# One core of a hybrid encoder: rows of the output projection through 32x32 transposes, and another order of the attention halves

## The chip, the cores and the metric

The kernel runs on one core of a Trainium2 chip, in one launch, all in float32 on the outside. The metric is the device time of one execution in microseconds (us); less is better. Engines are named as in the profile: PE (TensorE, with its weight loads as PEld), DVE (VectorE), ACT (ScalarE), POOL (GpSimd), SP (the queue that issues almost all transfers here).

## The reference, cut to what matters

One layer over 1024 rows of width 1024: RMSNorm, one wide projection, two mixers, the output projection with a residual, and an MLP of width 4096 with squared ReLU, then a final RMSNorm.

```
h = rmsnorm(x, norm_mix_g)
z = h @ w_in                      # q, k, v, g, a_f, a_b, su, sv
# mixer A, 4 heads, chunks of 64, forward and backward:
#   state_n+1 = dec_n * state_n + k_n v_n^T ; o = intra(q, k, v) + q_n state_n
o_gla = rmsnorm_head(o_f + o_b) * norm_g * silu(g)
# mixer B, 4 groups, chunks of 128:
o_sgu = gelu(su) * (w_s @ (rmsnorm_group(gelu(sv)) * norm_g) + b_s)
x = x + concat([o_gla, o_sgu]) @ w_out          # called x2 below
h = rmsnorm(x, norm_mlp_g)
x = x + square(relu(h @ w_mlp1)) @ w_mlp2
out = rmsnorm(x, final_norm_g)
```

## The kernel before

Every matmul operand is split into a high and a low part (`split`, L122: ACT writes the high part, DVE the difference), and each product is three matmuls of 128x512 on PE. Weight pieces of 128x512 come through `wpiece` (L132): a transfer by SP into a ring `wr` of two buffers, then the split into `wh` and `wl`, three buffers each.

**Recording and order.** The kernel is recorded in one pass. Instructions of PE keep the order in which they are recorded; those of the other engines are placed by a scheduler, which works with its own model of time and with priorities. The middle of the kernel is driven by a table of events: a generator `stream` records the projections in steps (mostly 12 matmuls, some 2.7 us of PE), and after step n every event with a number up to n is recorded. An event is one stage of one half (512 rows, `hf` 0 or 1) of one head `h`: gate, `st_cum` (cumulated decays), `st_score`, `st_tr`, `st_kv`, `st_attend`, `st_out`; and `sgu_mix`, the mixing matmuls of mixer B for one half and one group.

**State scan.** `st_kv` of the second half of a head runs two chains on DVE over the tile `X`: the forward one (L438) on the lower 64 partitions, and the backward one (L444) on the upper 64, which goes from chunk 14 down to chunk 1 and writes the state of the chunk before each. So the states of the second half of the rows are complete after six of its fourteen steps, those of the first half at its last step. `st_attend` multiplies masked scores `P` with `V` and then `qd` with the states `X` of its half. Its results go through ACT and POOL (norm) and DVE, and `st_out` transposes them back on PE and gates them into `V`. The tiles that PE writes here (`pg`) are a ring of four PSUM banks, handed out in the order of recording: a stage waits until the bank of four stages back has been read, mostly by DVE.

**Output projection.** It is computed transposed: for each of eight blocks `d` of 128 channels, 48 matmuls give two tiles of 128 channels x 512 rows, DVE adds the residual (`x2t[d, hf]`), and for each pair of blocks `x2_combine` (L650) makes the split operands of the MLP (a Winograd form, seven block products instead of eight). The MLP's end needs x2 also row by row, so `x2_natural` (L634) turns each tile with four PE transposes into a `pg` bank, copies it by ACT into a tile `st` of the ring `tmp` (two buffers) and stores it to DRAM as `x2n`, runs of 128 floats. It is recorded after the next block's matmuls; the last one after the first MLP pair (L809). `x2n` is read back by rows, first from L805.

**Start.** SP first loads a piece of `wv`, then `cols` (norm gains), then half a piece of x; the other half comes by ACT's queue (L176). The first matmul needs the split x (ACT, with a gain from `cols`) and the cast weight (DVE, L185).

Of the kernel before, what the change touches and what calls it, by code (L numbers as in the profile page):

```python
# [15 lines left out]
P = 128  # L16
# [15 lines left out]
def tile_encoder(  # L32
# [25 lines left out]
    nc = tc.nc  # L58
# [6 lines left out]
    def sb(tag, bufs, shape=(P, 512), dt=F32):  # L65
        cnt[0] += 1
        home = tiny if tag in ("sm", "rso", "r3") else pool
        return home.tile(list(shape), dt, tag=tag, bufs=bufs, name=f"{tag}{cnt[0]}")

    def one(name, shape, dt=F32):  # L70
        return tiny.tile(list(shape), dt, tag=name, bufs=1, name=name)

    def bank(tag, bufs=4):
        cnt[0] += 1
        return psum.tile([P, 512], F32, tag=tag, bufs=bufs, name=f"{tag}{cnt[0]}")
# [3 lines left out]
    def in_table_order(ins):  # L79

        if table["last"] is not None:
            tc.add_manual_dep(
                ins.ins,
                table["last"].ins.name,
                mybir.DependencyInfo(mybir.DependencyClass.NoSync, mybir.DependencyReason.DATA),
                reason="table order",
            )
        table["last"] = ins
# [11 lines left out]
    def pg():  # L100
        return bank("pg")
# [7 lines left out]
    def transp(o, i):  # L109
        tc.keep_in_program_order(nc.tensor.transpose(out=o, in_=i, identity=cid))  # L110

    def v3(ap, a):
        return ap.rearrange("p (a b) -> p a b", a=a)

    def bcast_in(ap, n):
        return ap[:, None, :].broadcast_to([ap.shape[0], n, ap.shape[1]])
# [15 lines left out]
    def wpiece(src):  # L132
        with tc.high_priority(offset=HP):
            raw = sb("wr", 2)
            nc.sync.dma_start(out=raw, in_=src)
            hi, lo = sb("wh", 3, dt=F32R), sb("wl", 3, dt=F32R)
            split(raw, hi, lo)
        return hi, lo
# [3 lines left out]
    ccols = one("cols", [P, 24])  # L142
# [12 lines left out]
    def in_order(ins, after):  # L155
        if after is not None:
            tc.add_manual_dep(
                ins.ins,
                after.ins.name,
                mybir.DependencyInfo(mybir.DependencyClass.NoSync, mybir.DependencyReason.DATA),  # L160
                reason="order of use",
            )
        return ins

    for k in range(KT):
        for hf in range(2):
            raw = sb("qk", 8)
            a, b = sb("xa", 16, dt=F32R), sb("xb", 16, dt=F32R)
            g = ccols[:, G1 + k : G1 + k + 1]
            xh[k, hf], xl[k, hf] = a, b  # L170
            if k == 0 and hf == 0:
                wraw = sb("wr", 2)
                whi, wlo = sb("wh", 3, dt=F32R), sb("wl", 3, dt=F32R)
                h0, h1 = slice(0, 256), slice(256, 512)
                with tc.high_priority(offset=1000):
                    first = nc.scalar.dma_start(out=raw[:, h0], in_=xT[0, :, h0])  # L176
                    table["last"] = in_order(
                        nc.scalar.preload_act_table_set("natural_log_exp_and_others"), first
                    )
                    table["logexp"] = True  # L180
                    in_table_order(nc.scalar.copy(out=one("wact", [P, 8]), in_=warm[:, 0:8]))
                    lead = nc.sync.dma_start(out=wraw, in_=wv[0])
                    lead = in_order(nc.sync.dma_start(out=ccols, in_=cols), lead)
                    lead = in_order(nc.sync.dma_start(out=raw[:, h1], in_=xT[0, :, h1]), lead)
                nc.vector.tensor_copy(out=whi, in_=wraw)  # L185
                in_table_order(nc.scalar.activation(out=a[:, h0], in_=raw[:, h0], func=AF.Copy, scale=g))
                nc.vector.scalar_tensor_tensor(
                    out=b[:, h0], in0=raw[:, h0], scalar=g, in1=a[:, h0].bitcast(F32), op0=ALU.mult, op1=ALU.subtract
                )
                nc.vector.tensor_tensor(out=wlo, in0=wraw, in1=whi.bitcast(F32), op=ALU.subtract)  # L190
                split(raw[:, h1], a[:, h1], b[:, h1], g)
                wvp.append((whi, wlo))
            else:
                nc.sync.dma_start(out=raw, in_=xT[k, :, hf * 512 : hf * 512 + 512])
                split(raw, a, b, g)
                if hf == 0:
                    wvp.append(wpiece(wv[k]))
# [63 lines left out]
    for hf in range(2):  # L261
        rb = pg()
        for i in range(4):
            t = hf * 4 + i
# [257 lines left out]
    def sgu_mix(hf, g):  # L522
        mx = pg()
        for i in range(4):
            mm(mx[:, i * P : i * P + P], SV[:, hf * 4 + i, g, :], cws[:, g * P : g * P + P], True, True)
        nc.vector.scalar_tensor_tensor(
            out=SV[:, hf * 4 : hf * 4 + 4, g, :], in0=v3(mx, 4), scalar=ccols[:, GS + g : GS + g + 1],
            in1=bcast_in(cbs[:, g * P : g * P + P], 4), op0=ALU.mult, op1=ALU.add,
        )
# [40 lines left out]
    ev = []  # L570
    for h in range(H):
        for hf in range(2):
            u = 2 * h + hf
            b0 = 7 + 6 * u
            for off, fn in ((-3 if u == 2 else -4, gate), (0, st_cum), (4, st_score), (5, st_tr), (7, st_kv)):
                ev.append((b0 + off, fn, h, hf))
            b1 = 7 + 6 * (2 * h + 1) + 11
            ev.append((b1 + hf, st_attend, h, hf))
            ev.append((b1 + 4 + hf, st_out, h, hf))
    for g in range(4):  # L580
        ev.append((21 + g, lambda hf, g: sgu_mix(hf, g), 0, g))
        ev.append((41 + g, lambda hf, g: sgu_mix(hf, g), 1, g))
    ev.sort(key=lambda e: e[0])
    pos = 0
    for _ in stream():
        pos += 1
        while ev and ev[0][0] <= pos:
            _, fn, h, hf = ev.pop(0)
# [6 lines left out]
    for src, base in ((SV, 4), (V, 0)):  # L595
        for j in range(4):
            for hf in range(2):
                a, b = sb("xa", 16, dt=F32R), sb("xb", 16, dt=F32R)
# [32 lines left out]
    x2n = dram.tile([NT, P, D], F32, name="x2n", tag="x2n", bufs=1)  # L631
    x2t = {}

    def x2_natural(d):  # L634
        for hf in range(2):
            tp = pg()
            for i in range(4):
                c = slice(i * P, i * P + P)
                transp(tp[:, c], x2t[d, hf][:, c])
            st = sb("tmp", 2)  # L640
            nc.scalar.copy(out=st, in_=tp)
            nc.sync.dma_start(
                out=x2n[hf * 4 : hf * 4 + 4, :, d * P : d * P + P].rearrange("t p c -> p t c"), in_=v3(st, 4)
            )


    XC = {n: {} for n in ("B11", "B21", "T2", "T1", "T3", "B22", "T4")}
# [30 lines left out]
    for n, d in enumerate(order):  # L678
        banks = [pf(), pf()]
        for p, k0 in ((1, 4), (0, 0)):  # L680
            hi, lo = wpiece(wo[d, p])
            for hf in range(2):
                for kk in range(4):
                    k = k0 + kk
                    a, b = hi[:, kk * P : kk * P + P], lo[:, kk * P : kk * P + P]
# [3 lines left out]
        for hf in range(2):  # L689
            with tc.high_priority(offset=HP):  # L690
                t = sb(("sg", "kn")[n % 2], 2)
# [258 lines left out]
    for p in range(NPAIR):  # L950
# [13 lines left out]
        if 2 <= p < 6:  # L964
            t = 2 + p
# [3 lines left out]
        if 9 <= p < 13:  # L969
            t = p - 9  # L970
# [57 lines left out]
    for tt in range(4):  # L1028
        t = 4 + tt
# [17 lines left out]
    for tt in range(4):  # L1047
        c = slice(tt * P, tt * P + P)
# [93 lines left out]
```

## Time and profile before

| what | us |
|---|---|
| median of 3 runs (lowest, highest) | 1019.59 (1015.92, 1019.97) |
| the profiled execution | 1017.8 |
| its span, first to last instruction | 1016.0 |
| PE busy in the span | 1000.5 (98%) |
| DVE busy | 693.0 (68%) |
| ACT busy | 474.0 (47%) |

The span is 1.8 us shorter than the time of its execution, and that execution lies 1.8 us below the median. PE is busy nearly always, at a granted clock of 0.995 on the mean; so what matters is what PE executes and the few places where it waits. The kernel's parts stand in the trace so: first projection to 48 us, the projections with both mixers to 303 us, output projection to 397 us, first MLP product to about 690 us, second to 1016 us.

### The profile page before, as it was taken

What the parts mean: (1) busy time and instruction counts of PE and PEld (TensorE: products, weight loads), DVE (VectorE), ACT (ScalarE), POOL (GpSimd) and SP (SyncE); (2) the same over time, 40 slices, a digit from 0 to 9 for tenths busy, and PEclk for the clock granted to TensorE, in tenths of its full rate; (3) what the DMA queues carried; (4) which work ended last, traced back from release to release, by engine and by line L of the source; (5) the groups of instructions that cost most, each with busy time, mean ns of one, the idle gap of its engine ahead of it and who ended that gap; (6) DMA issues with size and microseconds to landing.
All of it is one profiled execution on the core that took longest, in us unless ns stands there. A gap on an engine that the chain in (4) does not pass through costs nothing.

```text
span 1016.0 us, 14249 instructions
## 1 busy us (share of the span) xinstructions
PE 1000.5 (98%) x5014; PEld 825.1 (81%) x5014; DVE 693.0 (68%) x1178; ACT 474.0 (47%) x887; POOL 92.6 (9%) x101
## 2 busy tenths in 40 slices
PE   9999999898999999999999999999999999999997
PEld 7887888787888888888888888887888888788885
DVE  6245877776684557877677677665446776799684
ACT  6634646664464446434444433333444444445463
POOL 1001521342220000000000000000000000004031
PEclk9999999999999999999999999999999999999999
DMA  9422111110113444646446445226975652367342
GB/s 307 163 72 74 42 33 63 42 38 26 54 42 123 136 125 134 208 155 218 146 176 214 150 154 177 104 96 232 362 264 178 206 193 69 111 246 263 104 145 83
DMA packets 84984, 145.46 MB, mean 143 GB/s; under 512 B 8881, under 2 KB 17841, under 8 KB 84913
## 3 DMA queue, kind: packets, MB, share of 16 engines
q1 hardware_dynamic: 83760, 142.59, 41.8%
q10 hardware_dynamic: 1152, 1.97, 0.5%
q8 instruction: 39, 0.64, 0.3%
q14 instruction: 33, 0.26, 0.1%
HBM read 106.77 MB, written 37.75 MB: 142 GB/s over the span
## 4 chain that ended last, share of the span: by engine, by line
PE 92%; DVE 5%; ACT 1%; DMA 1%; issue 1%; SPq 0%; POOL 0%; POOLq 0%; DVEq 0%; ACTq 0%
PE pf L106 64%; PE pg L106 27%; PE pg L110 1%; DVE X L444 1%; DVE wl L125 1%; DVE X L438 1%; DMA k<-w 0%; DVE P L403 0%; DMA cols<-cols 0%; DMA wr<-wsv 0%; DVE qk L329 0%; DVE la L343 0%; DVE wl L628 0%; ACT wh L124 0%; DVE kin L382 0%
## 5 line engine op out<-in xcount | busy, mean ns | idle before, releaser
L106 PE MATMUL pg<-xa,xa 128*128 128x512 f32 x768 | 182.5, 390 | 0.4 <-DVE wh L628 0.2
L106 PEld LDWEIGHTS pg<-xa,xa 128*128 128x128 f32 x768 | 144.1, 188 | 31.0 <-DVE wh L628 0.7
L106 PE MATMUL pf<-xa,xa 128*128 128x512 f32 x576 | 138.8, 390 | 0.4 <-ACT kn L792 0.4
L106 PE MATMUL pf<-xa,wh 128*128 128x512 f32 x336 | 136.0, 405 | 0.0
L106 PE MATMUL pf<-xb,wh 128*128 128x512 f32 x336 | 131.9, 392 | 0.0
L106 PEld LDWEIGHTS pf<-xa,xa 128*128 128x128 f32 x576 | 108.0, 188 | 23.3 <-ACT kn L792 0.8
L106 PE MATMUL pf<-xa,wl 128*128 128x512 f32 x320 | 125.6, 393 | 0.0
L124 ACT CAST xa<-xb 128x512 fp32r<-128x512 f32 x76 | 47.1, 621 | 98.2 <-PE pf L106 74.8
L106 PE MATMUL pf<-V,xa 128*128 128x512 f32 x336 | 91.7, 389 | 0.0
L125 DVE TENSOR_TENSOR xa<-xb,xa 128x512 fp32r<-128x512 f32 x76 | 52.3, 689 | 52.8 <-ACT xa L124 52.6
L125 DVE TENSOR_TENSOR wl<-wr,wh 128x512 fp32r<-128x512 f32 x63 | 49.9, 793 | 50.1 <-ACT wh L124 49.8
L106 PEld LDWEIGHTS pf<-xa,wh 128*128 128x128 f32 x336 | 63.9, 190 | 13.9 <-issue 1.2
L941 POOL TENSOR_SCALAR r<-r 128x1 f32<-128x1 f32 x8 | 14.9, 1868 | 657.5 <-ACT tmp L939 657.3
L106 PEld LDWEIGHTS pf<-V,xa 128*128 128x128 f32 x336 | 63.1, 188 | 13.1
L106 PEld LDWEIGHTS pf<-xb,wh 128*128 128x128 f32 x336 | 63.8, 190 | 11.9
L106 PEld LDWEIGHTS pf<-xa,wl 128*128 128x128 f32 x320 | 60.5, 189 | 13.0
L124 ACT CAST wh<-wr 128x512 fp32r<-128x512 f32 x63 | 38.7, 615 | 63.6 <-PE pf L106 54.1
L124 ACT CAST xa<-k 128x512 fp32r<-128x512 f32 x49 | 30.5, 623 | 68.4 <-PE pf L106 66.4
L106 PE MATMUL pf<-xb,xa 128*128 128x512 f32 x192 | 53.9, 389 | 0.0
L106 PE MATMUL pf<-qk,xa 128*128 128x512 f32 x176 | 52.9, 390 | 0.0
L124 ACT CAST xa<-la 128x512 fp32r<-128x512 f32 x34 | 21.1, 622 | 46.5 <-PE pf L106 27.5
L106 PEld LDWEIGHTS pf<-xb,xa 128*128 128x128 f32 x192 | 36.1, 188 | 7.4
(296 smaller groups left out, 1840.4 us busy)
## 6 DMA issues: line engine op xcount, KB each, us to landing
k<-w SPq DMA_DIRECT2D x64, 256.0 KB, 3.1
hA<-kn SPq DMA_DIRECT2D x32, 256.0 KB, 3.1
hS<-wr SPq DMA_DIRECT2D x32, 256.0 KB, 4.3
la<-hA SPq DMA_DIRECT2D x17, 256.0 KB, 5.1
la<-hS SPq DMA_DIRECT2D x17, 256.0 KB, 2.7
qk<-xn SPq DMA_DIRECT2D x16, 256.0 KB, 5.5
wr<-wsv SPq DMA_DIRECT2D x16, 256.0 KB, 2.6
wr<-wo SPq DMA_DIRECT2D x16, 256.0 KB, 2.6
```

Of the source, the lines that this page charges most:

```text
L106: nc.tensor.matmul(out=o, lhsT=lhsT, rhs=rhs, start=start, stop=stop, skip_group_check=more)
L110: tc.keep_in_program_order(nc.tensor.transpose(out=o, in_=i, identity=cid))
L124: nc.scalar.copy(out=hi, in_=src)
L125: return nc.vector.tensor_tensor(out=lo, in0=src, in1=hi.bitcast(F32), op=ALU.subtract)
L438: nc.vector.scalar_tensor_tensor(out=x[lo64, n + 1, :], in0=x[lo64, n, :], scalar=sm[lo64, 2, i : i + 1], in1=v3(kv[i % 2], 4)[lo64, i // ...
L444: nc.vector.scalar_tensor_tensor(out=x[hi64, n - 1, :], in0=x[hi64, n, :], scalar=dec[h, n // 8][hi64, 2, n % 8 : n % 8 + 1], in1=x[hi64, ...
L941: nc.gpsimd.tensor_scalar(out=r[:, 4:5], in0=r[:, 0:1], scalar1=EPS, scalar2=None, op0=ALU.add)
```

## The change

Three edits. At the start, `cols` is loaded ahead of the first weight piece. In the table of events, the two halves of `st_attend` and of `st_out` of each head change places, and the mixing of group g moves from step 21+g to 30+g (first half) and from 41+g to 42+g (second half). In `x2_natural`, the four transposes on PE and the copy by ACT are replaced by one DVE instruction that transposes each 32x32 square of the tile in place of the whole; the four bands of 32 partitions of the result are then stored by a transfer each, which puts every run of 32 floats where it belongs.

```diff
-                    lead = nc.sync.dma_start(out=wraw, in_=wv[0])
-                    lead = in_order(nc.sync.dma_start(out=ccols, in_=cols), lead)
+                    lead = nc.sync.dma_start(out=ccols, in_=cols)
+                    lead = in_order(nc.sync.dma_start(out=wraw, in_=wv[0]), lead)
...
-            ev.append((b1 + hf, st_attend, h, hf))
-            ev.append((b1 + 4 + hf, st_out, h, hf))
+
+            ev.append((b1 + 1 - hf, st_attend, h, hf))
+            ev.append((b1 + 5 - hf, st_out, h, hf))
     for g in range(4):
-        ev.append((21 + g, lambda hf, g: sgu_mix(hf, g), 0, g))
-        ev.append((41 + g, lambda hf, g: sgu_mix(hf, g), 1, g))
+        ev.append((30 + g, lambda hf, g: sgu_mix(hf, g), 0, g))
+        ev.append((42 + g, lambda hf, g: sgu_mix(hf, g), 1, g))
...
         for hf in range(2):
-            tp = pg()
-            for i in range(4):
-                c = slice(i * P, i * P + P)
-                transp(tp[:, c], x2t[d, hf][:, c])
             st = sb("tmp", 2)
-            nc.scalar.copy(out=st, in_=tp)
-            nc.sync.dma_start(
-                out=x2n[hf * 4 : hf * 4 + 4, :, d * P : d * P + P].rearrange("t p c -> p t c"), in_=v3(st, 4)
-            )
+            nc.vector.transpose(out=st, in_=x2t[d, hf])
+            dst = x2n[hf * 4 : hf * 4 + 4, :, d * P : d * P + P].rearrange("t (a i) (b j) -> b i (t a) j", i=32, j=32)
+            for b in range(4):
+                nc.sync.dma_start(out=dst[b], in_=v3(st, 16)[b * 32 : b * 32 + 32])
```

Where the scheduler put things, as the order of the built programs tells it (no times are in it):

On PE, at the attention of the second head, the kernel before has these rows; `qd_1159` is made from the first half of the rows, `qd_1443` from the second, and `X_1457` holds the head's states:

```order
L106 MATMUL pg_1841<-V_490,P_1293 128x128 x4
L106 MATMUL pg_1841<-X_1457,qd_1159 64x128 x8
L110 MATMUL pg_1863<-ident,kd_1655 128x128 x4
...
L106 MATMUL pg_1890<-V_490,P_1576 128x128 x4
L106 MATMUL pg_1890<-X_1457,qd_1443 64x128 x8
L106 MATMUL pg_1912<-cuf,la_1733 64x128
```

and the kernel after these, with the states in `X_1433`; `qd_1419` is of the second half:

```order
L106 MATMUL pg_1841<-V_490,P_1552 128x128 x4
L106 MATMUL pg_1841<-X_1433,qd_1419 64x128 x8
L110 MATMUL pg_1863<-ident,kd_1637 128x128 x4
...
L106 MATMUL pg_1890<-V_490,P_1281 128x128 x4
L106 MATMUL pg_1890<-X_1433,qd_1159 64x128 x8
L106 MATMUL pg_1912<-cuf,la_1727 64x128
```

The halves have changed places; between them stand, in both, the transposes of `kd` and twelve matmuls of the projection.

On DVE, the later part of that head's scan stands so in the kernel before; `sm_1427` is the decay of the second half, `sm_1143` that of the first, L403 masks the scores of the next stage out of their `pg` bank:

```order
L438 SCALAR_TENSOR_TENSOR X_1457<-X_1457,sm_1427,pg_1677 64x128
L347 TENSOR_SCALAR tmp_1735<-la_1733 128x512
L444 SCALAR_TENSOR_TENSOR X_1457<-X_1457,sm_1427 64x128
...
L351 TENSOR_TENSOR la_1733<-la_1733,tmp_1735 128x512
L444 SCALAR_TENSOR_TENSOR X_1457<-X_1457,sm_1143 64x128 x2
L125 TENSOR_TENSOR wl_1978<-wr_1975,wh_1977 128x512
L444 SCALAR_TENSOR_TENSOR X_1457<-X_1457,sm_1143 64x128
L403 COPY_PREDICATED P_1777<-mkf,pg_1779 64x4x64 x2
L444 SCALAR_TENSOR_TENSOR X_1457<-X_1457,sm_1143 64x128
L403 COPY_PREDICATED P_1777<-mkb,pg_1780 64x4x64 x2
L444 SCALAR_TENSOR_TENSOR X_1457<-X_1457,sm_1143 64x128
```

and so in the kernel after, where L526 is the DVE part of `sgu_mix`:

```order
L438 SCALAR_TENSOR_TENSOR X_1433<-X_1433,sm_1403,pg_1665 64x128
L125 TENSOR_TENSOR wl_1804<-wr_1801,wh_1803 128x512
L444 SCALAR_TENSOR_TENSOR X_1433<-X_1433,sm_1403 64x128
L526 SCALAR_TENSOR_TENSOR V_579<-pg_1735,cols,k_577 128x4x128
L347 TENSOR_SCALAR tmp_1729<-la_1727 128x512
...
L351 TENSOR_TENSOR la_1727<-la_1727,tmp_1729 128x512
L444 SCALAR_TENSOR_TENSOR X_1433<-X_1433,sm_1143 64x128 x3
L125 TENSOR_TENSOR wl_1978<-wr_1975,wh_1977 128x512
L444 SCALAR_TENSOR_TENSOR X_1433<-X_1433,sm_1143 64x128
L403 COPY_PREDICATED P_1777<-mkf,pg_1779 64x4x64 x2
L403 COPY_PREDICATED P_1777<-mkb,pg_1780 64x4x64 x2
```

A mixing instruction has come into the scan (one more, L526 of `pg_1698`, stands near its start), and both pairs of L403 now follow its last step.

On SP, one block of the output projection in the kernel before; `wo` are weight pieces, `xT` the residual:

```order
L692 DMA sg_3164<-xT 128x512
L692 DMA sg_3167<-xT 128x512
L642 DMA x2n<-tmp_3091 128x4x128
L135 DMA wr_3311<-wo 128x512
L642 DMA x2n<-tmp_3099 128x4x128
L135 DMA wr_3341<-wo 128x512
```

and in the kernel after:

```order
L642 DMA x2n<-tmp_3166 32x16x32
L690 DMA kn_3240<-xT 128x512
L642 DMA x2n<-tmp_3166 32x16x32 x3
L135 DMA wr_3299<-wo 128x512
L690 DMA kn_3243<-xT 128x512
L642 DMA x2n<-tmp_3172 32x16x32 x4
L135 DMA wr_3329<-wo 128x512
```

Where six transfers were issued for a block there are twelve, and the loads of weights and residual stand among the stores. The DVE transposes (L639) stand directly behind, or within four instructions of, the addition that makes their tile, ahead of later weight splits.

## Rows read from the trace of the kernel before

**Rows 1.** The page: busy time by engine, and the chain that ended last by engine.

```profile
PE 1000.5 (98%) x5014; PEld 825.1 (81%) x5014; DVE 693.0 (68%) x1178; ACT 474.0 (47%) x887; POOL 92.6 (9%) x101
...
PE 92%; DVE 5%; ACT 1%; DMA 1%; issue 1%; SPq 0%; POOL 0%; POOLq 0%; DVEq 0%; ACTq 0%
```

**Rows 2.** Who PE waited for, 100 to 260 us: total, times, longest.

```profile
PE pg L106 <- DVE X L444: 5.5, 2, 2.9
PE pg L106 <- DVE la L343: 0.6, 1, 0.6
```

**Rows 3.** PE in order of time: start, us, what, [idle before, and until what].

```profile
189.47 1.50 PE L106 MATMUL pg<-X,qd 128*64 128x128 f32 x16 [2.65 <-DVE X L444]
...
196.29 1.09 PE L106 MATMUL pg<-X,qd 128*64 128x128 f32 x16
```

**Rows 4.** The chain from 185 to 200 us: start, us, what.

```profile
189.47 1.50 PE pg L106 x16
190.98 1.04 PE pg L110 x4
192.02 3.45 PE pf L106 x12
```

**Rows 5.** The chain from 200 to 440 us.

```profile
208.44 0.44 PE pg L110 x4
...
244.84 1.05 PE pg L110 x4
245.89 3.82 PE pf L106 x12
...
252.50 2.95 PE pf L106 x12
...
325.40 0.87 PE pg L110 x8
```

**Rows 6.** A 5 us stretch: PE, PEld, DVE, ACT, POOL, then PE clock, DMA share, GB/s.

```profile
190.00:195.00 5.00, 5.00 (x27) 4.08 (x22) 3.29 (x6) 3.47 (x12) 1.21 (x2) 0.66 0.17 54
```

**Rows 7.** DVE in the scans of the first and second head.

```profile
131.14 0.75 DVE L526 SCALAR_TENSOR_TENSOR V<-pg,cols,k 128x512 f32<-128x512 f32 x1
...
181.75 0.35 DVE L444 SCALAR_TENSOR_TENSOR X<-X,sm 64x128 f32<-64x128 f32 x1
...
188.26 0.91 DVE L403 COPY_PREDICATED P<-mkb,pg 64x256 f32<-64x256 uint8 x2
189.07 0.35 DVE L444 SCALAR_TENSOR_TENSOR X<-X,sm 64x128 f32<-64x128 f32 x1
```

**Rows 8.** Two blocks of the output projection, columns as in rows 6.

```profile
325.40:337.17 11.77, 11.77 (x58) 9.84 (x57) 8.79 (x15) 7.09 (x13) 0.00 (x0) 1.00 0.45 134
337.17:348.94 11.77, 11.77 (x59) 9.84 (x57) 3.27 (x6) 4.28 (x8) 0.00 (x0) 1.00 0.41 134
```

**Rows 9.** DVE on 128x512: count, ns min/median/max, first and last start.

```profile
L628 DVE TENSOR_TENSOR tmp<-pf,wl x16: 681/692/692, 414.0 to 699.8; 128x512 f32<-128x512 f32 x16
...
L347 DVE TENSOR_SCALAR tmp<-la x8: 406/418/448, 68.7 to 234.6; 128x512 f32<-128x512 f32 x8
```

**Rows 10.** Transfers of 24 to 34 us.

```profile
DMA packets 2170, 3.95 MB, mean 395 GB/s; under 512 B 245, under 2 KB 245, under 8 KB 2169
...
q1 hardware_dynamic: 2169, 3.94, 103.1%
```

**Rows 11.** Transfers of 384.5 to 396.5 us.

```profile
DMA packets 1344, 1.05 MB, mean 87 GB/s; under 512 B 64, under 2 KB 1088, under 8 KB 1344
...
q1 hardware_dynamic: 1344, 1.05, 27.9%
```

**Rows 12.** Issue of one store of x2n by SP.

```profile
338.54 0.38 SPq L642 DMA_DIRECT2D x2n<-tmp  x1
```

**Rows 13.** The chain at the start.

```profile
1.16 3.03 DMA cols<-cols
```

**Rows 14.** DVE at the start.

```profile
3.88 0.57 DVE L185 CAST wh<-wr 128x512 fp32r<-128x512 f32 x1 [3.88 <-DMA wr<-wv]
```

## What the change is predicted to do

> **What bounds the kernel now.** I read the busy shares first: PE has 1000.5 us of work in a span of 1016.0, DVE 693.0, ACT 474.0, and the chain that ended last is PE for 92% and DVE for 5% [rows 1]. The reader is to see that an edit pays here only through what PE executes on that path, and through PE's waits. So I read next for whom PE waits in the mixers, where the table of events is changed: 5.5 us in two waits for the scan (`X`, L444), 0.6 us in one for a gate (`la`, L343) [rows 2]. Then the timeline and the chain around these waits [rows 3 to 7], one block of the output projection [rows 8], and the transfers [rows 10 to 12].
>
> The profiled execution took 1017.8 us (span 1016.0 and 1.8 around it). The sum is made against it; the median of the runs, 1019.59, lies 1.8 higher.
>
> **The order of the halves and the mixing.** In the second head PE is ready for `X` at 189.47 − 2.65 = 186.82 and waits until the scan's last step, 189.07 + 0.35 = 189.42 [rows 3, 7]. But it asks there for the first half, which comes last. The second half's states are complete with the sixth backward step, at 181.75 + 0.35 = 182.10 [rows 7], 4.7 us before PE is ready. So the first attend of the changed kernel doesn't wait. The question is the second one, which now wants the first half.
>
> PE comes to it, counted from 186.82, after an undisturbed attend (1.09), four transposes (0.44) and twelve matmuls (2.95) [rows 3, 5]: 191.3 at the earliest; the `V,P` matmuls ahead of it, and the mixings that now stand before this place, make it later. DVE's scan gets two mixing operations of 0.75 us more and loses the pairs of L403, which stand behind it now; but PE's bank waits for the first of these pairs. One pair takes 0.91 [rows 7]: 189.42 + 2 × 0.75 − 0.91 = 190.0. That leaves 1.3 us. In the third head PE's attend begins at 244.84 − 1.50 = 243.3 after 2.9 us of waiting [rows 2, 3, 5], so it was ready at 240.4 and wants the first half at 244.9; the scan by the same sum is ready at 243.9, 1.0 us earlier. Both waits go: 5.5 us. The first and the fourth head have no such wait before, and none is late enough to get one.
>
> After each of the two stalls the same work takes longer. In the stretch behind the first, PE's granted clock is 0.66 of full speed [rows 6], between its two levels of 1.2 and 2.4 GHz, after 2.65 us without work. The attend takes 1.50 instead of 1.09, the transposes 1.04 instead of 0.44, the twelve matmuls 3.45 instead of 2.95: 1.5 us [rows 3 to 5]. Behind the second the transposes take 1.05 and the twelve matmuls 3.82: 1.5 us [rows 5], the attend not counted. Without a stall the clock has no reason to fall: 3.0 us more.
>
> The 0.6 us wait for a gate belongs to a mixing at step 21 that claims a bank that the gate has not released; with the mixing at step 30 that neighbour is gone. This part gives 5.5 + 3.0 + 0.6 = 9.1 us. The DVE work of the mixing is only moved.
>
> **The rows of the output projection: PE.** Of 64 transposes, eight go together, 0.87 us on the chain [rows 5], eight times: 7.0 us. In a block of 11.77 us PE is busy for 11.77 [rows 8], so nothing else is late there, and a block becomes 10.90. The ACT copies go too, from an engine that is busy for 7.09 and 4.28 of 11.77 us and not on the chain: nothing.
>
> **DVE.** Two transposes of 128x512 per block come in. The trace doesn't show the operation. From below it costs what a one-input operation on this shape takes, 0.42 us; from above, say twice the slowest comparable row, 1.4 us; I take the nearest, 0.69, of a two-input operation [rows 9], since nothing in the trace shows how a square is turned. Blocks carry 8.79 and 3.27 us of DVE work in turn [rows 8]; with 1.4 us more they are 10.2 and 4.7 of 10.9. With 2 × 1.4 the heavy block is 11.6, over its time by 0.7, but two blocks hold 8.79 + 3.27 + 4 × 1.4 = 17.7 of 21.8, and the light one takes up the rest if the splits that DVE makes have so much lead. Cover: DVE's idle time in the light block. The transposes stand right behind the residual additions, and each waits until four stores of the tile two before have landed, one block earlier; behind it on DVE wait the weight splits, and PE for these. A block of 10.9 us is long for landing stores if transfers are not full; that is the next point. The Trainium skill, "VectorE: DVE Perf Modes", section "The three transpose paths", gives 311 ns for 128x128 in bf16 (in squares of 32x32 only); four of them would be 1.24 us, an estimate that no run here shows, two blocks would hold 17.0 of 21.8, and the sum would be the same.
>
> **Transfers.** SP issues twelve transfers a block where it issued six; at 0.38 each [rows 12] that is 4.6 of 10.9 us: nothing, as long as none blocks. The stores' runs shrink from 512 to 128 bytes: 8192 packets become 32768, per block 4096, or 256 on each of 16 engines. The price of such a packet is not in the trace. Where loads of 2 KB fill the engines, 24 to 34 us, 1.031 × 10 × 16 = 165 engine-us over 1924 large packets (2169 − 245) are 86 ns each [rows 10]. At the end of the output projection, 384.5 to 396.5, 0.279 × 12 × 16 = 53.6 engine-us hold 256 packets of 2 KB (22.0) and 1024 of 512 bytes: 31 ns each [rows 11]. A straight line through the two gives 17 ns for 128 bytes, which I take as the lower end, and no gain from shorter runs, 31 ns, as the nearest row. Twice that row, 62, for a short run that is handled in two passes, is the upper end. I take 25, between the line and the row. Per block each engine also carries four loads, 8 packets of 86 ns each, 2.7 us. So the engines are busy for 2.7 + 256 × 0.025 = 9.1 of 10.9 us; at 17 ns 7.1, at 31 ns 10.6, at 62 ns 18.6. It decides from (10.9 − 2.7)/256 = 32 ns. Below that the stores lie beside PE: nothing.
>
> **The start.** `cols` lands at 1.16 + 3.03 = 4.19 [rows 13]; a place earlier it comes by about one issue, 0.4 us, sooner, the weight by as much later. The cast of the weight now runs 3.88 to 4.45 [rows 14]. One of the two operands of the first matmuls gains what the other loses: I take 0; bounds −0.4 and +0.4.
>
> **Sum.** 9.1 + 7.0 + 0 = 16.1: 1017.8 − 16.1 = 1001.7 against the profiled execution, 1019.6 − 16.1 = 1003.5 against the median. I say 1002.5, with its own range of 999 to 1006 (the start, the stretch after stalls, waits of tenths that come anew, and which of the two executions is typical).
>
> **Rivals.**
>
> Second: the waits stay or come back elsewhere. The margins of 1.3 and 1.0 us rest on sums over moved DVE work; if the scheduler's order delays the scan by more (a weight split of 0.7 us and a mixing more), PE waits for the first half, and its clock falls behind the wait. For it: three kinds of DVE work share this stretch, all placed by a model. Against it: `V,P` matmuls and mixings not counted in PE's favour. Only the 7.0 us of the transposes come: 1010.8 against the profile, 1012.6 against the median.
>
> Third: DVE becomes the bound in the output projection. Transposes near 1.4 us, waiting in order for stores, delay splits, and the 7.0 us are lost there while the 9.1 come: 1008.7 to 1010.5. For it: 8.79 us in a heavy block. Against it: 3.27 in the next.
>
> Fourth, on the other side: the short runs make the transfers the bound of the output projection. Its place is SP's order, where weight loads stand among stores, so that PE waits for `wo`. From 32 ns a packet a block grows by 0.256 us for each ns; over eight blocks the 16.1 us saved are used up at about 40 ns ((10.9 − 2.7 + 16.1/8) / 256). At 50 ns a block takes 15.5, 4.6 more than 10.9: eight of them +37, 1017.8 − 16.1 + 37 = 1038.7; at 62 ns +62, 1063. For it: four times as many packets in a direction (store, strided) for which only 512-byte runs are shown. Against it: from 2 KB to 512 bytes the price fell from 86 to 31 ns, so size still counted at 512. The Trainium skill, "DMA: Bandwidth & Descriptors", Specifications, speaks for this rival: below 512 bytes a transfer reads, modifies and writes, and does not reach line rate. No run here shows a run of 128 bytes that fills the engines.
>
> **How the numbers follow.** The forecast 0.68; waits that stay 0.12; DVE bound 0.08; transfers bound 0.12. Up to 1012.5 lie the first, the third and most of the second, so 998 to 1012.5 holds some 0.82; what is left out is nearly all the fourth, which alone would widen the range by 50 us. A measurement of this kernel tells about 0.5% from no change, some 5 us: faster is below 1014.5. The forecast (0.68), the third (0.07) and two thirds of the second (0.08) are faster: 0.83. The rest of these and prices of 37 to 42 ns a packet are no change: 0.06. Higher prices are slower: 0.11.
>
> **What would show it.** Right: no wait of PE for `X`, a granted clock of 1.00 from 185 to 250 us, blocks of 10.9 us in the output projection with no transposes in the chain, a DVE transpose at 0.7 us, store packets at 25 ns and a DMA share of 0.8 to 0.9 in the blocks. Wrong: PE waiting for `X`, or for a bank that L403 reads, at the second attend; DVE waiting for `x2n` stores and PE for `wl` behind it; a DMA share of 1.00 and PE waiting for `wo` loads.

## The result and the profile after

The changed kernel takes 1001.67 us (median of 5 runs, 1001.23 to 1002.07) against 1019.17 (5 runs, 1015.92 to 1019.97): ratio 0.9833, 95% interval 0.9817 to 0.9849. The forecast was 1002.5, its range 998 to 1012.5. The profiled execution took 1002.07 us, span 1000.3, 15.7 less than the span before.

The page after, beside [rows 1]: busy time by engine, then the chain that ended last by engine.

```profile
PE 989.8 (99%) x4950; PEld 815.5 (82%) x4950; DVE 700.8 (70%) x1194; ACT 467.8 (47%) x871; POOL 93.3 (9%) x101
...
PE 97%; DMA 1%; DVE 1%; ACT 0%; SPq 0%; POOL 0%; issue 0%; POOLq 0%; DVEq 0%
```

PE has 64 instructions and 10.7 us less; DVE, with 16 instructions more, is still at 70%. The chain is PE for 97% instead of 92%.

All that PE waited for in the whole span (total us, times, longest), beside [rows 2]:

```profile
PE pg L106 <- POOL tmp L147: 1.3, 1, 1.3
PE pf L106 <- ACT xa L127: 0.6, 1, 0.6
PE pf L106 <- DVE xb L128: 0.3, 1, 0.3
PE pg L106 <- DVE wh L629: 0.2, 1, 0.2
PE pf L106 <- DVE wh L185: 0.2, 1, 0.2
PE pg L106 <- DVE wl L629: 0.2, 1, 0.2
```

Neither the scan (`X`) nor the gate (`la`) is in it: no wait at all in the mixers. Two waits at the start of the kernel, 0.6 and 0.3 us, are for the second piece of x; the section on the start comes back to them.

The two stretches that held the stalls, columns as in [rows 6]:

```profile
185.00:195.00 10.00, 10.00 (x89) 8.59 (x89) 7.59 (x18) 8.59 (x27) 3.08 (x8) 1.00 0.18 54
195.00:250.00 55.00, 55.00 (x411) 45.37 (x410) 40.37 (x87) 32.07 (x59) 22.05 (x21) 1.00 0.11 30
```

PE is busy all the time at a granted clock of 1.00, where [rows 6] had 0.66.

The chain from 300 to 420 us, beside [rows 5], then two blocks of the output projection, beside [rows 8]:

```profile
299.99 84.77 PE pf L106 x374
```

```profile
311.00:321.90 10.90, 10.90 (x50) 9.03 (x49) 7.59 (x12) 5.00 (x8) 0.00 (x0) 1.00 0.58 139
...
332.80:343.70 10.90, 10.90 (x50) 9.03 (x49) 7.73 (x13) 5.10 (x8) 0.00 (x0) 1.00 0.71 155
```

The transposes that interrupted the chain every 10.9 us are gone, and blocks follow each other in 10.90 us. Over six blocks, 311 to 376.4 us, DVE has 6.9 to 9.0 us of work in each, more evenly spread than the 8.79 and 3.27 of before, and the transfers are busy for 0.58 to 0.71 in five of them and 0.33 in the last, below the 0.8 to 0.9 that the prediction named as a sign. Of the signs against it one came, once, and at no cost: at the last transpose, 406.6 us, DVE waits for a store, and PE for nothing behind it.

```profile
DVE tmp L639 <- DMA x2n<-tmp: 2.3, 1, 2.3
```

The new DVE instruction (eight of the sixteen; the others have the same times; count, ns min/median/max, first and last start), and the transfers of 311 to 376.4 us, beside [rows 11]:

```profile
L639 DVE STREAM_TRANSPOSE tmp<-sg x8: 702/708/712, 303.9 to 373.6; 128x512 f32<-128x512 f32 x8
```

```profile
DMA packets 28487, 8.75 MB, mean 134 GB/s; under 512 B 25788, under 2 KB 25788, under 8 KB 28482
...
q1 hardware_dynamic: 28482, 8.68, 59.5%
```

A transpose takes 0.708 us, where 0.69 was taken. Of the transfers, 0.595 × 65.4 × 16 = 623 engine-us hold 2694 large packets at 86 ns (232) and 25788 small ones: 15 ns each. The forecast took 25, with 17 as the lower end.

Where the time went is read from two marks on PE, the first transposes of `kd` and the first matmul of the first MLP product (here the first of the two kernels is before, the second after; count, ns, first and last start):

```profile
L110 PE MATMUL pg<-ident,kd x32: 270/272/477, 93.8 to 269.6; 128*128 128x128 f32 x32
...
L106 PE MATMUL pf<-V,xa x336: 388/389/390, 398.8 to 701.4; 128*128 128x512 f32 x168
```

```profile
L110 PE MATMUL pg<-ident,kd x32: 270/272/329, 94.9 to 261.0; 128*128 128x128 f32 x32
...
L106 PE MATMUL pf<-V,xa x336: 389/389/389, 383.9 to 685.6; 128*128 128x512 f32 x168
```

Up to the first mark the changed kernel is 1.1 us later. Between the marks it takes 289.0 instead of 305.0 us, 16.0 less, of which seven of the eight groups of transposes are 6.1 and the mixers 9.9. PE's busy time tells what the 9.9 are (the stretch between the marks, before and after, columns as in [rows 6]):

```profile
93.80:398.80 305.00, 298.88 (x1882) 246.58 (x1881) 205.92 (x405) 162.44 (x308) 57.73 (x58) 0.99 0.22 68
94.90:383.90 289.00, 289.00 (x1826) 238.16 (x1825) 211.87 (x417) 155.73 (x293) 57.11 (x58) 1.00 0.28 73
```

PE stood still for 6.1 us before and not at all after. Its work fell by 9.9 with 56 instructions fewer, the seven groups of transposes at 6.1; so the instructions that are in both kernels took 3.8 us less.

### The profile page after: what moved, and what is told of

Same layout as the page of the kernel before. It is cut to its first block, busy times and chain, and to the rows that moved or that the text cites. A ratio compares the mean times of both kernels' runs of the same rounds, so it can differ in the third digit from the quotient of the medians.

```text
span 1000.3 us, 14178 instructions
## 1 busy us (share of the span) xinstructions
PE 989.8 (99%) x4950; PEld 815.5 (82%) x4950; DVE 700.8 (70%) x1194; ACT 467.8 (47%) x871; POOL 93.3 (9%) x101
## 4 chain that ended last, share of the span: by engine, by line
PE 97%; DMA 1%; DVE 1%; ACT 0%; SPq 0%; POOL 0%; issue 0%; POOLq 0%; DVEq 0%
PE pf L106 68%; PE pg L106 28%; PE pg L110 1%; DMA qk<-xT 1%; DMA R<-w 0%; DVE wl L629 0%; DVE xa L125 0%; DVE k L629 0%; ACT xa L124 0%; POOL r L941 0%; DVE xb L128 0%; ACT xa L127 0%; DVE wh L629 0%; POOLq L1136 0%; ACT tmp L937 0%
## 5 line engine op out<-in xcount | busy, mean ns | idle before, releaser
L939 POOL TENSOR_SCALAR r<-r 128x1 f32<-128x1 f32 x8 | 16.3, 2031 | 648.7 <-ACT tmp L937 648.5
```

What stands on the lines that cost most here:

```text
L939: nc.gpsimd.tensor_scalar(out=r[:, 4:5], in0=r[:, 0:1], scalar1=EPS, scalar2=None, op0=ALU.add)
```

## The experiments

All medians in us; the ratio is to the kernel before in the same set of runs. The changed kernel, 1001.67, is what each is compared with; it was run in one set only, and the kernel before had medians of 1017.44 to 1019.17 in the four sets, so differences of less than about a microsecond between medians tell nothing.

| run | median (lowest, highest) | ratio, 95% interval | PE's waits in the mixers |
|---|---|---|---|
| e1 events undone | 1010.81 (1010.12, 1011.84) | 0.9929, 0.9915 to 0.9943 | X 5.5, la 0.6 |
| e2 rows undone | 1008.79 (1007.74, 1009.58) | 0.9908, 0.9894 to 0.9922 | none |
| e3 start undone | 1002.68 (1000.98, 1003.32) | 0.9843, 0.9827 to 0.9858 | none |
| e4 exchange alone | 1006.38 (1006.09, 1007.28) | 0.9883, 0.9868 to 0.9898 | V (L476) 2.5, la 0.6 |
| e5 mixing alone | 1005.21 (1004.50, 1005.76) | 0.9868, 0.9852 to 0.9884 | X 3.2 |
| e6 stores twice | 1002.16 (1001.64, 1002.68) | 0.9840, 0.9820 to 0.9860 | none |
| e6 stores four times | 1042.94 (1041.74, 1044.14) | 1.0240, 1.0217 to 1.0264 | none |
| e7 transposes twice | 1002.19 (1001.35, 1003.03) | 0.9852, 0.9832 to 0.9872 | none |
| e7 transposes four times | 1007.03 (1006.60, 1007.47) | 0.9900, 0.9880 to 0.9920 | none |
| e8 start, loads pinned | 1001.36 (1001.25, 1001.45) | 0.9836, 0.9822 to 0.9849 | none |
| e9 mixing, second half moved | 1002.98 (1002.02, 1003.95) | 0.9860, 0.9845 to 0.9875 | la 0.6 |
| e10 mixing, first half moved | 1003.72 (1003.10, 1004.30) | 0.9869, 0.9852 to 0.9885 | V (L476) 1.2 |

The time between the two marks above leaves the start and its spread out. It is 289.0 us in the changed kernel, 297.2 in e1, 295.3 in e2, 292.5 in e4, 292.3 in e5, 289.9 in e9 and 290.3 in e10, one execution each.

**Each part undone by itself.** e1 takes the table of events of before:

```diff
-            ev.append((b1 + 1 - hf, st_attend, h, hf))
-            ev.append((b1 + 5 - hf, st_out, h, hf))
+            ev.append((b1 + hf, st_attend, h, hf))
+            ev.append((b1 + 4 + hf, st_out, h, hf))
...
-        ev.append((30 + g, lambda hf, g: sgu_mix(hf, g), 0, g))
-        ev.append((42 + g, lambda hf, g: sgu_mix(hf, g), 1, g))
+        ev.append((21 + g, lambda hf, g: sgu_mix(hf, g), 0, g))
+        ev.append((41 + g, lambda hf, g: sgu_mix(hf, g), 1, g))
```

> The changed kernel (1001.7 us) with the table of events of before: halves and mixing back in their places; rows and start as changed. Theory: the parts add up, and the order of events carries 9.1 us or a little more (5.5 of waits, 3.0 to 3.8 of slow matmuls behind them, 0.6 for the gate): 1010.8 to 1011.6 us, with two waits of PE for X (L444) of 2.5 to 3 us each and a granted clock near 0.66 behind them. Rival: only the waits themselves count and the slower clock is made up later: 1007.2. Rival: the mixers' gain came from elsewhere (the scheduler's new placement of everything): 1002 to 1005.

It gives 9.1 us back, and PE's waits of before are there again. PE in order of time, at the two stalls, and the stretch of 5 us behind each (its granted clock stands third from the end):

```profile
190.22 1.09 PE L106 MATMUL pg<-X,qd 128*64 128x128 f32 x16 [2.60 <-DVE X L444]
...
242.92 1.18 PE L106 MATMUL pg<-X,qd 128*64 128x128 f32 x16 [2.90 <-DVE X L444]
```

```profile
190.20:195.20 5.00, 4.98 (x39) 4.30 (x40) 3.24 (x5) 4.05 (x13) 1.21 (x2) 1.00 0.23 54
242.90:247.90 5.00, 4.98 (x29) 4.10 (x30) 1.73 (x3) 3.54 (x11) 1.82 (x3) 0.66 0.19 52
```

The waits are those expected; the slow stretch behind them came once and not twice. Behind 2.65 us without work ([rows 3], [rows 6]) and behind 2.9 us (here, and at the second stall of the kernel before) the clock was at 0.66 in the next 5 us; behind 2.60 us it was at 1.00. The theory's 9.1 us for the whole part holds for the time; its share for the clock is not the same in every execution.

e2 takes the rows of before:

```diff
-            st = sb("tmp", 2)
-            nc.vector.transpose(out=st, in_=x2t[d, hf])
-            dst = x2n[hf * 4 : hf * 4 + 4, :, d * P : d * P + P].rearrange("t (a i) (b j) -> b i (t a) j", i=32, j=32)
-            for b in range(4):
-                nc.sync.dma_start(out=dst[b], in_=v3(st, 16)[b * 32 : b * 32 + 32])
+            tp = pg()
+            for i in range(4):
+                c = slice(i * P, i * P + P)
+                transp(tp[:, c], x2t[d, hf][:, c])
+            st = sb("tmp", 2)
+            nc.scalar.copy(out=st, in_=tp)
+            nc.sync.dma_start(
+                out=x2n[hf * 4 : hf * 4 + 4, :, d * P : d * P + P].rearrange("t p c -> p t c"), in_=v3(st, 4)
+            )
```

> The changed kernel (1001.7 us) with the rows of the output projection as before: PE transposes, ACT copies, 16 stores in runs of 512 bytes; events and start as changed. Theory: 64 transposes, 7.0 us, come back on PE: 1008.7 us, blocks of 11.77 us. Rival: some of the saving is lost again to DVE, ACT or the stores in the changed kernel (SP waits, later splits): the rows are worth only 3 to 5 us, 1004.7 to 1006.7.

1008.79: 7.1 us come back, and the chain shows them as in [rows 5]:

```profile
315.67 0.87 PE pg L110 x8
316.54 10.90 PE pf L106 x48
```

So the parts add up: 9.1 and 7.1 are 16.2, of 17.5 between the medians (16.0 against the kernel before in the runs of e1 and e2, 1017.69). The rest, −0.2 to +1.3 us, lies in the start and in the spread.

**The start.** e3 puts the weight piece first again; e8 keeps the gains first, but records the third weight piece ahead of the third full piece of x, makes that piece follow it on SP, and holds constants back, so that SP's loads come nearly in the order of before:

```diff
-                    lead = nc.sync.dma_start(out=ccols, in_=cols)
-                    lead = in_order(nc.sync.dma_start(out=wraw, in_=wv[0]), lead)
+                    lead = nc.sync.dma_start(out=wraw, in_=wv[0])
+                    lead = in_order(nc.sync.dma_start(out=ccols, in_=cols), lead)
```

> The changed kernel (1001.7 us) with the first weight piece ahead of the gains again; all else as changed. Theory: the changed start costs 1.1 us (the first matmuls begin 0.45 us earlier at the second one, but PE then waits 0.9 us for the second piece of x, which lands at 7.8 us): 1000.6 us, first projection ending 1.1 us earlier. Rival: the 1.1 us is variation of the first loads from one execution to the next: 1001.7, and the profile may show either.

```diff
+                if (k, hf) == (1, 1):
+                    wvp.append(wpiece(wv[2]))
+                ld = nc.sync.dma_start(out=raw, in_=xT[k, :, hf * 512 : hf * 512 + 512])
+                if (k, hf) == (1, 1):
+                    in_order(ld, wload["last"])
+                if (k, hf) == (5, 0):
+                    held = ld
...
+    for c, src in ((cid, ident), (cuf, cumf), (cub, cumb)):
+        in_order(nc.sync.dma_start(out=c, in_=src), held)
```

> The changed kernel (1001.7 us), gains first, but the loads that SP issues behind are pinned to the order of the kernel before (third weight piece ahead of the third piece of x, constants later). Theory: what is lost at the start is not the gains' place but the five pieces of x issued in a row, which all share the transfers with the one that PE needs next; pinned, the second piece lands before 6.6 us, no wait, and the start is 0.45 us better than before: 1000.1 us. Rival: the weight issued 0.44 us later is what is late: PE waits as in the changed kernel, 1001.7.

e3 was 1.0 us above the changed kernel, not 1.1 below, and its runs spread over 2.3 us. The expected cost of the changed start is not there. PE in order of time, after:

```profile
5.18 0.49 PE L106 MATMUL pf<-wh,xb 128*128 128x512 f32 x1
...
8.61 0.49 PE L106 MATMUL pf<-wh,xa 128*128 128x512 f32 x1 [0.65 <-ACT xa L127]
9.39 0.50 PE L106 MATMUL pf<-wh,xb 128*128 128x512 f32 x1 [0.29 <-DVE xb L128]
```

In e3:

```profile
5.63 0.79 PE L106 MATMUL pf<-wh,xb 128*128 128x512 f32 x1
...
8.78 0.63 PE L106 MATMUL pg<-wh,xa 128*128 128x512 f32 x1
9.58 0.39 PE L106 MATMUL pf<-wl,xa 128*128 128x512 f32 x1
```

With the gains first PE starts its second matmul 0.45 us earlier in these two executions, and then waits 0.9 us for a piece of x. In e3 it has no such wait, but its first matmuls take 0.63 us or more each until 9.2 us, where 0.39 is usual; in the kernel before they had come down to 0.39 by 6 us. So executions of one and the same start differ by more than the edit: `kd` first comes at 93.8 in the kernel before, 95.6 in e3. The other experiments leave the changed start as it is, and their traces say the same: in the eleven profiled executions that have it, `kd` first comes between 93.8 (e2) and 95.2 (e4), and PE's waits for x are 0.2 us in e2 and none in e10. The 1.1 us of the first pair of profiles is within that spread.

In e8 the second piece of x was being split at 6.8 us instead of 7.8, and PE's waits for it were gone, as the theory says; its median, 0.3 us lower, cannot be told from the changed kernel. What the start is worth stays open within about a microsecond.

**What the mixing's move is for.** e4 keeps the mixing at its old steps, e5 keeps the halves at their old places: of e1's diff, the last four lines or the first four.

> The changed kernel (1001.7 us), but the mixing stays at its old steps (21+g and 41+g): only the halves of attend and out have changed places. Theory: the exchange alone takes both waits for X and the slow matmuls behind them away, and the mixing's move is worth only the 0.6 us of the gate: 1002.3 us, no wait of PE for X, one of 0.6 us for la (L343). Rival: the mixing ahead of PE's second attend is what gives the first half its time; without it PE waits again for X, with the slow stretch behind: 1004 to 1008.

> The changed kernel (1001.7 us), but the halves of attend and out keep their old places: only the mixing is moved. Theory: the waits for X stay and with two mixing operations inside the scan of the second head one of them grows by up to 1.5 us, less what the mixings' matmuls on PE take up: 1010.2 to 1011.5 us. Rival: the moved mixing fills PE's waits (16 matmuls, some 1.8 us, stand ahead of the attend of the second head now): 1006 to 1008.

Of the first theory only the mechanism of the exchange holds: in e4 no wait for `X` is left. But the time is 4.7 us above the changed kernel, not 0.6. The rival gave the time, and not the reason: what came in the place of the scan is the mixing itself. The waits in e4:

```profile
PE pg L106 <- DVE V L476: 2.5, 1, 2.5
...
PE pg L106 <- DVE la L343: 0.6, 1, 0.6
```

PE in order of time, then DVE:

```profile
205.33 0.60 PE L110 MATMUL pg<-ident,tmp 128*128 128x128 f32 x4
...
208.54 0.60 PE L110 MATMUL pg<-ident,tmp 128*128 128x128 f32 x4
209.07 0.69 PE L106 MATMUL pg<-qin,kin 64*64 64x64 f32 x32
212.30 1.13 PE L106 MATMUL pg<-k,V 128*128 128x128 f32 x8 [2.54 <-DVE V L476]
```

```profile
211.40 1.41 DVE L476 SCALAR_TENSOR_TENSOR V<-pg,cols,sg 128x512 f32<-128x512 f32 x2 [1.25 <-ACT sg L95]
```

The name is misleading, here and in what was expected of e9 and e10: `V` in the wait is what L476 writes, not what PE reads. L476 is DVE's part of `st_out`; it reads a `pg` bank and gates it into mixer A's `V`. The rows that the mixing reads are another tile of the same name, normalised by POOL (L517):

```profile
200.80 4.04 POOL V L517 x4
```

They are done at 204.84, before PE asks at 209.76. What PE lacks is a bank, as with the gate: four stages back in the ring stand the transposes of the second half's `st_out` (205.33; then those of the first half, and the scores with two banks), and their bank is free after the first L476, at 212.1. No run gives the mixing another bank, so this is read from the order of recording and the trace. With the halves in their old places the bank at that point is the first half's: in the kernel before L476 is done with it at 210.8, and PE comes at 212.64, after the stall of the second head. With the exchange PE comes 2.9 us earlier and the bank 1.3 us later, because the second half's `st_out`, now the first, waits for its gate (`sg`, ACT L95). One step later, at 42, the transposes of `kd` claim that bank first, twelve matmuls further on: in the changed kernel it is free at 209.7, and PE is there at 211.40.

In e5 the stall of the second head is gone too, without the exchange; four mixings, moved to steps 30 to 33, stand on PE ahead of that attend now. The first head has lost them, and has a wait for `X` now, 1.8 us; the other one of the two, 1.3, is in the third head. The two theories were both too simple; 1005.2 lies below either.

e9 and e10 move the mixing of one half each:

```diff
-        ev.append((30 + g, lambda hf, g: sgu_mix(hf, g), 0, g))
+        ev.append((21 + g, lambda hf, g: sgu_mix(hf, g), 0, g))
```

> The changed kernel (1001.7 us), but the mixing of the first half stays at steps 21+g; that of the second half is moved by its one step, 41+g to 42+g. Theory: with the scan's wait gone PE comes to step 41 before the normalised rows V (L476) are ready, and the one step is what covers that (with the exchange alone: a wait of 2.5 us and slow matmuls, 1006.4). So this kernel has no wait for V and only the 0.6 us for la: 1002.3 us. Rival: the nine steps of the first half are what carries the rest (they keep PE longer before the second head's attend): 1005 to 1006.4, with the wait for V.

```diff
-        ev.append((42 + g, lambda hf, g: sgu_mix(hf, g), 1, g))
+        ev.append((41 + g, lambda hf, g: sgu_mix(hf, g), 1, g))
```

> The counterpart: the changed kernel (1001.7 us), first half's mixing at 30+g, second half's at 41+g as before. Theory: the wait for V (L476) at step 41 stays, 1.1 us by the times of the changed kernel (PE there at 208.5, V from 209.7) to 2.5 us as with the exchange alone, with up to 1.5 us of slow matmuls behind it: 1003 to 1005.7 us, no wait for la. Rival: no wait, 1001.7.

Both came as the theory said, though the wait is for a bank and not for rows. With the second half's mixing one step later there is no wait for L476, and `la`'s 0.6 us stands alone (1.3 us over the changed kernel). With it at step 41, PE waits for L476 even when the first half has been moved:

```profile
209.58 1.13 PE L106 MATMUL pg<-k,V 128*128 128x128 f32 x8 [1.20 <-DVE V L476]
```

So by the medians the step from 41 to 42 is worth 2.1 us with the first half moved (e10) and 3.4 with it left (e4 against e9); the nine steps of the first half are worth 1.3, and both together 4.7. Between the marks it is 1.3, 2.6, 0.9 and 3.5. Either way the parts add up to less than the whole: with neither moved (e4) PE asks for the bank at 209.8 and has it at 212.3, with the first half moved (e10) at 208.4 and 209.6. So L476 itself comes later in e4; which of the engines in the chain to its gate is the reason wasn't tried.

**How far the transfers and DVE are from binding.** e6 writes each store again into one or three copies that nothing reads, the second and fourth by ACT's queue in the larger one; e7 does each transpose two or four times.

```diff
-            for b in range(4):
-                nc.sync.dma_start(out=dst[b], in_=v3(st, 16)[b * 32 : b * 32 + 32])
+            for to in [x2n] + x2c:
+                dst = to[hf * 4 : hf * 4 + 4, :, d * P : d * P + P].rearrange("t (a i) (b j) -> b i (t a) j", i=32, j=32)
+                for b in range(4):
+                    nc.sync.dma_start(out=dst[b], in_=v3(st, 16)[b * 32 : b * 32 + 32])
```

> The changed kernel (1001.7 us) with each store of the rows done twice, the second time into a copy that nothing reads: 8192 packets of 128 bytes per block of the output projection instead of 4096. Theory, from the trace after (a packet of 128 bytes takes some 15 ns): 2.7 + 512 x 0.015 = 10.4 us of transfers in a block of 10.9, the queue of SP issues 20 transfers in it: no change to +4, 1001.7 to 1006 us. Rival, by the 25 ns of the prediction: 15.5 us a block, 4.6 over in eight blocks: 1038.

> The changed kernel (1001.7 us) with each store of the rows done four times, three of them into copies that nothing reads, half of all issued by ACT's queue: 16384 packets of 128 bytes per block. Theory, at 15 ns: 2.7 + 1024 x 0.015 = 18.1 us of transfers a block, 7.2 over in eight blocks: the transfers bind, 1059 us. Rival, at 25 ns: 28.3 a block, 1141. Rival, the issue binds first (32 stores a block on two queues at 0.4 to 0.5 us): about 8 us on each queue, not binding. The packet's time is read from the stretch in which the transfers are full.

Twice the packets change nothing that the spread would let show; the rival by 25 ns falls. Transfers of 330 to 380 us in that kernel:

```profile
DMA packets 40146, 8.93 MB, mean 179 GB/s; under 512 B 38105, under 2 KB 38105, under 8 KB 40142
...
q1 hardware_dynamic: 40142, 8.88, 88.4%
```

0.884 × 50 × 16 = 707 engine-us, less 2037 large packets at 86 ns (175): 14 ns for each of 38105. Four times the packets cost 41 us, 1042.94, slower than the kernel before. PE's longest waits there, a stretch in which the transfers are full and PE stands still, and ACT's queue:

```profile
PE pf L106 <- ACT V L124: 20.2, 1, 20.2
PE pf L106 <- ACT wh L760: 7.7, 2, 6.2
PE pf L106 <- ACT wl L768: 4.3, 1, 4.3
```

```profile
390.00:400.00 10.00, 0.00 (x0) 0.00 (x0) 2.08 (x3) 0.00 (x0) 0.00 (x0) 0.50 1.29 181
```

```profile
382.99 17.98 ACTq L644 DMA_DIRECT2D x2c<-tmp  x23
```

The transfers of 330 to 380 us in it:

```profile
DMA packets 50842, 9.65 MB, mean 193 GB/s; under 512 B 49115, under 2 KB 49115, under 8 KB 50838
```

That the transfers are full is shown: their share is 1.05 to 1.34 in every 10 us from 310 to 420. The path to PE is not the fourth rival's. PE keeps its pace up to 383 us, while work lies ready, and never waits for `wo`; it waits at the first MLP product for operands that ACT makes, and ACT stands for 17.9 of those 20.2 us behind 23 stores in its own queue, where this experiment put them. What four times the packets would cost with all stores on SP isn't shown. 1059 was expected, 16 us more. A share above 1 says that the times of packets overlap, so that the sum of their times overstates what they cost: in the full stretch of 330 to 380 us 49115 small packets and 1723 large ones went through 16 engines, which leaves at most 13.3 ns of an engine for each small one. With that the expectation's sum would be 16.3 us a block, 43 us over in eight blocks: an estimate near the 41 measured.

```diff
-            nc.vector.transpose(out=st, in_=x2t[d, hf])
+            for _ in range(2):      # 4 in the larger one
+                nc.vector.transpose(out=st, in_=x2t[d, hf])
```

> The changed kernel (1001.7 us) with each of the 16 DVE transposes done twice, into the same tile: what the upper end of the prediction, 1.4 us, would have meant. Theory: DVE has 7.7 + 2 x 0.71 = 9.1 us of work in a block of 10.9 on the mean, and its idle time covers it: 1001.7. Rival (DVE binds in the heavy blocks, splits come late): 1003 to 1008.

> The changed kernel (1001.7 us) with each of the 16 DVE transposes done four times: 7.7 + 6 x 0.71 = 12.0 us of DVE work for a block of 10.9. Theory: now DVE binds, about 1 us over in each of the six to eight blocks, less what is made ahead: 1003 to 1010, with PE waiting for splits (wl, L125). Rival: DVE's lead over PE is large enough that nothing shows: 1001.7.

At twice the price, the prediction's upper end, DVE still covers it. At four times DVE is late, and PE waits for splits, but not the weights' (`wl`) as expected. A block, and the 5 us behind the waits (columns as in [rows 6], DVE third), and what PE waited for:

```profile
321.90:332.80 10.90, 10.90 (x49) 9.03 (x49) 10.90 (x19) 5.70 (x10) 0.00 (x0) 1.00 0.51 116
...
392.86:397.86 5.00, 5.00 (x15) 3.97 (x16) 4.84 (x8) 1.73 (x3) 0.00 (x0) 0.66 0.63 160
```

```profile
PE pf L106 <- DVE V L125: 1.8, 1, 1.8
...
PE pf L106 <- ACT V L124: 0.8, 1, 0.8
```

DVE is busy all the time in two of six blocks, and PE isn't slowed in any of them. It pays at the first MLP product, where operands (in a tile named `V`) come late, 2.6 us in two waits, and its granted clock is at 0.66 behind them.

## Why the prediction was right, point by point

**The rows, 7.0 us: right.** The blocks went from 11.77 to 10.90, and undoing this part alone costs 7.1 us.

**DVE, 0.69 us a transpose: right**, 0.708, and with room: twice as much changes nothing. The Trainium skill, "VectorE: DVE Perf Modes", section "The three transpose paths", led to an estimate of 1.24 us; the measurement differs and decides, 0.708 for this shape in float32.

**Transfers, 25 ns a packet: too high, without effect on the sum.** 14 to 15 ns were measured, below the lower end, 17, and so the share in the blocks stayed below the 0.8 to 0.9 that was to show it. The straight line through two sizes came nearer than the row that it was leaned towards. The point of decision, 32 ns, was more than twice the real price, which e6 shows: at twice the packets nothing, at four times the transfers are full. At 128 bytes in 14.5 ns an engine moves 8.8 GB/s, at 2 KB in 86 ns 23.8. The rule of the Trainium skill, "DMA: Bandwidth & Descriptors", Specifications, that runs below 512 bytes miss the line rate, agrees with that, though at 512 bytes in 31 ns, 16.5 GB/s, the 2 KB packet's rate isn't reached either; that they would be read, modified and written is not seen in the price, since the shorter packet was the cheaper one.

**The order, 9.1 us: right in the sum, wrong in its split, and in part by luck.** Undoing the part costs 9.1. The two waits for `X` went as worked out, 5.5 us, though the sum for the third head took the attend there at 1.50 us, where the trace of the kernel before has 1.13, and so dated PE's arrival 0.4 us too early. Between the marks the mixers gained 9.9 in the profile: 6.1 of waits, and 3.8 of instructions that took less time, 3.0 of which the prediction had counted. The clock's share is a size that varies, one slow stretch in the profile of e1 and two before.

The term that was mis-sized is the mixing, put at 0.6 us for the wait for a gate. With the exchange in place the mixing's move is worth 3.5 us between the marks and 4.7 by the medians: besides the gate's wait it takes away one for the bank of the second half's `st_out`. The prediction asked what is late next only at the attends, not at the next stage that needs a bank, 20 us on; had the change had the exchange alone, it would have been 3 to 4 us too low. That the change had the covering step in it, and the prediction didn't know what it was for, is luck. The second rival, waits that come back elsewhere, is what e4 and e5 show, each with one half of this edit.

**The start, 0 with bounds of 0.4 us: not settled.** In the profiled execution it was 1.1 us late, outside the bounds. The bounds left out that the scheduler moves the loads behind, by which the second piece of x came a microsecond later in that execution. But executions of one start differ as much, 93.8 to 95.2 us at the first `kd`, and neither e3 nor e8 can be told from the changed kernel.

## What to carry to other kernels

- A stall that is removed lets the bounding engine arrive earlier everywhere behind it. Ask what is late next at each operand and each bank that this engine needs until the slack is larger than the gain, not only at the place of the stall. The tile that a profile names in a wait is what the releasing instruction writes; the reason can be what that instruction reads.
- Two edits of one table are tested apart in both ways: each alone and each left out. Here exchange (4.4) and mixing (5.6) together gave 9.1 with quite different waits taken away.
- A price that the profile doesn't show can be bounded by doubling the thing: twice the stores and twice the transposes at no cost showed the room that the estimates left open. The copies have to go where the originals go: those on ACT's queue in e6 blocked ACT, which the change never does.

## What the runs showed of the hardware

- Store packets of 128 bytes took 14 to 15 ns on a transfer engine, of 512 bytes 31, of 2 KB 86.
- A DVE transpose of 128x512 in float32, by squares of 32x32, took 0.70 to 0.71 us.
- After 2.60 us without matmuls PE's granted clock stayed at 1.00 (e1), and after 2.54 too (e4). After 2.65 us (before) and 2.9 us (before, e1) it was 0.66 in the next 5 us, and so it was after two shorter waits, 0.83 and 1.84 us with one matmul between them that took 0.50 us (e7 at four times). These cases give no rule.
- The second piece of x was issued at 2.57 or 2.58 us in every run. In the eleven executions with four more pieces behind it in a row it was split from 6.75 to 8.15 us (7.83 in the changed kernel); in the three with one behind it (before, e3, e8) from 6.48, 6.72 and 6.82.
